# A mixer, differential attention and a second mixer on one core: the order of the first block, and which queue loads the low-rank weights

## The chip, the cores and the metric

One NeuronCore of one Trainium2 chip runs the whole program in one launch. The metric is the time on the device in us, the median over the runs shown. "TensorE" is PE in the rows, "VectorE" DVE, "ScalarE" ACT, "Pool" POOL, and "SP" the queue of the sync engine, which only issues transfers here.

## The reference

The input x has 256 tokens of 2048 channels. Layer A is an RWKV-7 mixer with a residual layer norm, layer B differential attention with another, block C a sparse attention and retention mixer with a squared-relu MLP. The change lies in layer A alone, up to its eighth head group:

```
xx = shift(x) - x
xs = x[None] + xx[None] * mu_proj[:, None, None, :]
r, k, v, g = einsum('sbtd,sde->sbte', xs, w_in)
xw = x + xx * mu_lora[0];  xa = x + xx * mu_lora[1]
w_log = -softplus(-(w0 + tanh(xw @ w1) @ w2)) - 0.5;  decay = exp(-exp(w_log))
a  = sigmoid(a0 + (xa @ a1) @ a2)
kk = normalised(k * k_k);  k = k * (1 + (a - 1) * k_a)
S_t = S_{t-1} diag(w_t) - (S_{t-1} kk_t) (a_t*kk_t)^T + v_t k_t^T ;  y_t = S_t r_t
y = groupnorm(y) + bonus;  x = layernorm(ALPHA * x + (y * silu(g)) @ w_out)
```

All of it is float32; the kernel makes each product with the weights from two float32r parts of both sides.

## The kernel before

Activations are kept transposed, each as a high part xh and a low part xl. `dense` (L210) makes one block of 512 output columns for both token tiles of 128. SP loads the raw weights in pairs of k-tiles, 512 KB each, into four buffers. For each of the 16 k-tiles ScalarE casts the high part wh (L221), VectorE subtracts it to get the low part wl (L222), both with four buffers, and TensorE makes six products (L230, L231, L232 for each token tile): 96 products to a block. Between k-tiles `dense` calls a hook and takes pieces of other work from two lists, `soon` and `side`.

Layer A has 16 blocks: r (0 to 3), k (4 to 7), v (8 to 11) and g (12 to 15). The mixed input of the r blocks is made ahead of and beside block 0 by `mixed` (L419): pairs of k-tiles are mixed from x and from the steps xxg by two operations on VectorE (ms, L410), cast by ScalarE (xh, L166) and subtracted by VectorE (xl, L167). Pool makes three of the four granules of xxg (L399, L400). The low-rank hidden layers tanh(xw @ w1) and xa @ a1 are sixteen pieces in `side` (`low_rank`, L486), which run from block 1 on: each loads 128 KB of weights, issued by ScalarE (L488), casts and splits them (L490, L491), mixes a pair of k-tiles and makes six products.

Beside the v and g blocks run eight head groups ("head 0" to "head 7", four heads each). `wkv_prepare` loads rkl (r, k and kk, 768 KB) and w2 ([97, 2, 256], 194 KB), makes zp, the product of the hidden layer with w2 (L602), the sigmoid sig (ScalarE L605, VectorE L606), its parts sh and sl (L608, L609), the sums over chunks (L618 with the mask tri, a cast of trif), the decays E, then KB and ZR, the masked products AT (L662, L664), and the blocks of the inverse. These pass through DRAM to Pool, which substitutes (L690, L692), and come back as xd; L733 is the first product that needs them. The third mixed input, for the g blocks, is made again from x, which `mixed_again` loads in pairs (xt, L446) for VectorE's xx (L448).

A tile scheduler orders the instructions of each engine, apart from those marked to be kept in program order, and places transfers and casts ahead of the place where they stand in the program when their buffers are free. In the kernel before, nothing below was marked: the loads by ScalarE of tables, id16, trif, kkb, rkl and w2 could be moved ahead.

Of the kernel before, what the change touches and what calls it, by code (L numbers as in the profile page):

```python
# [17 lines left out]
D = 2048  # L18
T = 256
# [7 lines left out]
PLAN = 203.0            # weight of the steps of the heads over the blocks beside which they are put  # L27
SP = ((0.0, 0.2), (0.2, 0.8), (0.6, 0.8))     # their parts of a period
PAUSE = 8.0             # weight of the step that waits for the value blocks
AHEAD = 2               # pairs of k-tiles that are mixed before the first block  # L30
LAG = 10                # k-tiles by which the first token tile leads in the blocks around a norm


# ---------------------------------------------------------------- constants of the shapes
def const_tables():
# [13 lines left out]
    # distance of query and key, very large where the chunk mask forbids the pair  # L49
# [7 lines left out]
    # rotary tables, token-major  # L57
# [5 lines left out]
    # retention decay, key rows by query columns: blocks (0,0) (0,1) (1,1)  # L63
# [15 lines left out]
    # T5 buckets of the distances 255 - i, one-hot; row 32 marks the masked (negative) ones  # L79
# [16 lines left out]
def body(tc, I, out, dbg=None, stop=99):  # L96
# [3 lines left out]
    with ExitStack() as ctx:  # L100
# [29 lines left out]
        def load(pool, name, src, shape, eng=None, **kw):  # L130
            t = pool.tile(shape, F32, tag=name, name=name, **kw)
            (eng or S).dma_start(t, src)
            return t

        def bc_rows(src, n):
            """An AP that reads the n contiguous values at src for each of 128 partitions."""
            return bass.AP(tensor=src.tensor, offset=src.offset, ap=[[0, 128], [1, n]])
# [4 lines left out]
        S.copy(warm, mhalf)                         # the activation tables come in beside the first loads  # L142
        lnc = cst.tile([128, 15, KT], F32, name="lnc")              # vectors by channel

        def rpow(dst, src, n):
            """dst = src ** -0.5 for a few values per partition."""
            G.tensor_tensor(dst, src, mhalf.to_broadcast([128, n]), op=OP.pow)
# [4 lines left out]
        # ------------------------------------------------ matrix products with the weights  # L152
        class HL:
            """Activations, transposed, as two float32r parts whose sum is the float32 value."""
# [14 lines left out]
        def tok_to_hl(hlx, g, src, tts=(0, 1)):  # L169
            """src: token-major [128, 2, 512]; fills granule g."""  # L170
# [15 lines left out]
        def stepped(steps):  # L186
            """The steps of a generator, one at a time, as work for `side`."""

            def go():
                if next(steps, "end") is None:  # L190
                    side.insert(0, go)

            return go

        def in_turn(gens):
            """The steps of several generators, each a step behind the one before."""
# [12 lines left out]
        def dense(hlx, w, n=512, ks=None, hook=None):  # L209
            """One block of output columns, for both token tiles; returns the two PSUM tiles.  # L210
            Between its steps it emits the work that stands in `soon`, then in `side`."""
# [26 lines left out]
        # ------------------------------------------------ norms between products  # L238
        def norm_between(hlo, w, evac, finish, hlx, src, gain, offset, w_next, wp):
            """The four blocks hlo @ w, a norm of the rows that leads to src, and hlx = src * gain + offset  # L240
            (by channel) with the first block hlx @ w_next, whose PSUM tiles it returns.
            evac(tt, j, acc) takes a block in, finish(tt) makes src for one token tile."""
# [35 lines left out]
        def residual_ln(res_block, dst):  # L278
            """The two functions of norm_between for the layer norm of (ALPHA * residual + block)."""
# [19 lines left out]
        def gain_rows(dst, gain, offset, after=None):  # L299
            """dst = dst * gain + offset in place, row by row; gain and offset by their quarters of columns."""  # L300
# [12 lines left out]
        def rows_of(tiles, src):  # L313
            """Rows of D values broadcast over the partitions, in the given places; returns its quarters."""
# [5 lines left out]
        def pairs(t):  # L320
            """The 512-wide pairs that fit in a tile, as places for split weights."""
# [5 lines left out]
        def lag_block(hlx, w, store, hooks, place=0):  # L327
            """One block of output columns, the first token tile some k-tiles ahead of the second, so that
            what follows from one token tile runs beside the products of the other. store holds split weights."""
# [38 lines left out]
        # ================================================ layer A: RWKV-7  # L368
        vo = res.tile([128, 2, D], F32, tag="r1", name="vo")          # v, then the mixer's output
# [5 lines left out]
        with ExitStack() as actx:  # L375
# [5 lines left out]
            # the input, channel-major, and the steps to the tokens before; the places are the heads' later  # L381
# [37 lines left out]
            def mixed(which, ahead=8):  # L419
                """The mixed input in two parts. Returns it and a hook for the first block that uses it,  # L420
                which makes the parts beyond the first `ahead` pairs of tiles."""
                hx = HL()

                def pair(q):
                    if q % 2 == 0:
                        hx.alloc(q // 2)
                    split_from(hx, q // 2, slice(2 * (q % 2), 2 * (q % 2) + 2), slice(0, T), mix_pair(which, q))

                left = list(range(ahead, 8))
                calls = [0]  # L430

                def hook():
                    calls[0] += 1
                    if left and calls[0] % 2:
                        pair(left.pop(0))

                for q in range(ahead):
                    pair(q)
                return hx, hook

            def mixed_again(which):
                """The same when the input has left its places."""
# [15 lines left out]
            # r, k and the normalised k * k_k: channel-major, kept in DRAM until their heads come up  # L458
            rkd = [da.tile([128, 3, 4, T], F32, name=f"rkd{j}") for j in range(4)]
            hx, ahead = mixed(0, AHEAD)  # L460
# [19 lines left out]
            # low-rank hidden layers, rank by token, a few products at a time between those of the blocks  # L480
# [4 lines left out]

            def low_rank(q, li):  # L486
                w1 = ap1.tile([128, 2, 128], F32, tag="pr", name="lw1")
                S.dma_start(w1, I[("w1", "a1")[li]][:, 2 * q:2 * q + 2])  # L488
                wp = ap1.tile([128, 2, 2, 128], FR, tag=("f", "tha")[li], name="lwp")
                S.copy(wp[:, 0], w1)  # L490
                V.tensor_sub(wp[:, 1], w1, wp[:, 0].bitcast(F32))  # L491
# [15 lines left out]
            r_block(0, ahead)  # L507
# [11 lines left out]
            V.tensor_scalar(a0h, lnc[:, 12], 0.5, None, op0=OP.mult)  # L519
            V.tensor_scalar(kah, lnc[:, 13], 0.5, None, op0=OP.mult)  # L520
            V.tensor_scalar(kab, kah, -1.0, 1.0, op0=OP.mult, op1=OP.add)
            rkm = ap1.tile([128, KT, 2], F32, name="rkm")
            V.memset(rkm, 0.0)
            V.tensor_copy(rkm[0:64, :, 0], lnc[0:64, 14])
            V.tensor_copy(rkm[64:128, :, 1], lnc[64:128, 14])
# [3 lines left out]
            def k_block(j):  # L529
                acc = dense(hx, I["w_k"][j])  # L530
                kkb = ap1.tile([128, 512], F32, tag="xx", name="kkb")
                S.dma_start(kkb, bc_rows(I["k_k"][512 * j:512 * j + 512], 512))
# [32 lines left out]
            # v: token-major  # L565
# [14 lines left out]
            S.dma_start(trif, I["consts"][:, _OFF["tri"][0]:_OFF["mask_a"][0]])  # L580
            S.copy(tri, trif)
            # block-diagonal inverses pass through DRAM; the zeros around the blocks are written once
# [959 lines left out]
```

## Time and profile before

| | us |
|---|---|
| median of 3 runs | 2468.78 |
| lowest, highest | 2464.99, 2470.33 |
| span of the profiled execution, first to last instruction | 2472.8 |
| TensorE busy in it | 2392.2 (97%), 12378 matmuls |
| VectorE busy | 1540.1 (62%) |
| ScalarE busy | 1240.3 (50%) |
| Pool busy | 322.1 (13%) |

The mean granted clock of TensorE over the profiled execution is 0.983 of full speed. The span of the profiled execution is 4.0 us longer than the median of the runs; its own time on the device, what lies around the span included, is not among the times shown. In the page's table by 40 slices of 61.8 us TensorE is busy six tenths of the first slice and of the fifth (from 247 us), eight tenths of two others, and nine or more of the rest. The rows are read so: a stretch is found in the table of windows, the cause of a gap in the bracket behind the row that ends it, and the time of a transfer in the views of the transfers.

### The profile page before, as it was taken

What the parts mean: (1) busy time and instruction counts of PE and PEld (TensorE: products, weight loads), DVE (VectorE), ACT (ScalarE), POOL (GpSimd) and SP (SyncE); (2) the same over time, 40 slices, a digit from 0 to 9 for tenths busy, and PEclk for the clock granted to TensorE, in tenths of its full rate; (3) what the DMA queues carried; (4) which work ended last, traced back from release to release, by engine and by line L of the source; (5) the groups of instructions that cost most, each with busy time, mean ns of one, the idle gap of its engine ahead of it and who ended that gap; (6) DMA issues with size and microseconds to landing.
All of it is one profiled execution on the core that took longest, in us unless ns stands there. A gap on an engine that the chain in (4) does not pass through costs nothing.

```text
span 2472.8 us, 34618 instructions
## 1 busy us (share of the span) xinstructions
PE 2392.2 (97%) x12378; PEld 1940.8 (78%) x12378; DVE 1540.1 (62%) x2679; ACT 1240.3 (50%) x2540; POOL 322.1 (13%) x455
## 2 busy tenths in 40 slices
PE   6999699999999999999989999999999999999998
PEld 4887577777787788888878887878788888888886
DVE  6777466655466755776575477665655555556555
ACT  3555343435446455555464445455655555445443
POOL 1013244334400400100030011000000000000001
PEclk9999898989999999999999999999999999999999
DMA  5777534444365766546656754456566666666664
GB/s 183 213 231 253 146 96 125 121 103 96 95 208 179 216 189 194 145 145 182 198 179 197 243 150 137 128 174 210 166 184 186 187 189 186 187 187 187 187 188 154
DMA packets 155862, 428.08 MB, mean 173 GB/s; under 512 B 47110, under 2 KB 51294, under 8 KB 155049
## 3 DMA queue, kind: packets, MB, share of 16 engines
q1 hardware_dynamic: 139680, 386.84, 53.3%
q0 software_dynamic: 6128, 23.65, 3.3%
q10 hardware_dynamic: 9880, 15.39, 2.0%
q8 instruction: 97, 1.59, 0.3%
q14 instruction: 77, 0.62, 0.1%
HBM read 413.20 MB, written 14.18 MB: 173 GB/s over the span
## 4 chain that ended last, share of the span: by engine, by line
PE 88%; DVE 5%; DMA 3%; issue 1%; ACT 1%; POOL 1%; POOLq 0%; DVEq 0%; SPq 0%; ACTq 0%
PE acc L230 24%; PE acc L231 23%; PE acc L232 23%; PE m L150 3%; PE acc L341 2%; PE acc L339 2%; PE acc L340 2%; PE m L733 1%; PE m L662 1%; DVE wl L222 1%; PE m L776 1%; PE m L801 1%; PE m L765 1%; PE m L769 1%; DMA lw<-in_a 1%
## 5 line engine op out<-in xcount | busy, mean ns | idle before, releaser
L222 DVE TENSOR_TENSOR wl<-raw,wh 128x512 fp32r<-128x512 f32 x1312 | 916.8, 703 | 694.6 <-ACT wh L221 690.9
L221 ACT CAST wh<-raw 128x512 fp32r<-128x512 f32 x1312 | 811.8, 621 | 878.7 <-PE acc L232 524.3
L230 PE MATMUL acc<-wh,xh 128*128 128x512 f32 x2624 | 1058.3, 403 | 18.1 <-ACT wh L221 18.1
L231 PE MATMUL acc<-wl,xh 128*128 128x512 f32 x2624 | 1036.5, 395 | 9.4 <-DVE wl L222 9.4
L232 PE MATMUL acc<-wh,xl 128*128 128x512 f32 x2624 | 1036.7, 395 | 0.0
L230 PEld LDWEIGHTS acc<-wh,xh 128*128 128x128 f32 x2624 | 495.8, 189 | 128.5 <-ACT wh L221 20.1
L231 PEld LDWEIGHTS acc<-wl,xh 128*128 128x128 f32 x2624 | 496.8, 189 | 115.4 <-DVE wl L222 12.8
L232 PEld LDWEIGHTS acc<-wh,xl 128*128 128x128 f32 x2624 | 495.8, 189 | 110.9 <-issue 0.9
L1447 POOL TENSOR_TENSOR dn<-dn,gd 128x512 f32<-128x512 f32 x6 | 9.4, 1578 | 672.0 <-ACT jk L1446 672.0
L690 POOL TENSOR_TENSOR pr<-A,X 64x15 f32<-64x15 f32 (+7 forms) x120 | 50.2, 418 | 197.8 <-DMA A<-d 189.2
L359 DVE TENSOR_TENSOR lw<-raw,lw 128x512 fp32r<-128x512 f32 x84 | 56.4, 700 | 29.9 <-ACT lw L358 29.5
L358 ACT CAST lw<-raw 128x512 fp32r<-128x512 f32 x84 | 50.4, 629 | 42.8 <-PE acc L341 28.0
L341 PE MATMUL acc<-lw,xl 128*128 128x512 f32 x168 | 67.6, 402 | 3.8 <-DVE xl L167 3.7
L339 PE MATMUL acc<-lw,xh 128*128 128x512 f32 x168 | 68.7, 409 | 2.3 <-ACT xh L166 2.3
L340 PE MATMUL acc<-lw,xh 128*128 128x512 f32 x168 | 67.0, 399 | 0.0
L772 ACT COPY Q<-m 64x256 f32<-64x256 f32 x32 | 11.8, 368 | 79.1 <-PE m L769 75.9
L662 PE MATMUL m<-ZR,KB 64*128 64x128 f32 x256 | 39.7, 311 | 6.2 <-DVE KB L647 6.2
L662 PEld LDWEIGHTS m<-ZR,KB 64*128 64x128 f32 x256 | 33.0, 208 | 14.0 <-issue 7.9
L692 POOL TENSOR_TENSOR X<-X,pr 64x15 f32<-64x15 f32 (+7 forms) x120 | 42.0, 350 | 9.2
L341 PEld LDWEIGHTS acc<-lw,xl 128*128 128x128 f32 x168 | 32.1, 191 | 13.1 <-DVE xl L167 6.1
L167 DVE TENSOR_TENSOR xl<-m,xh 128x512 fp32r<-128x512 f32 (+1 forms) x60 | 36.7, 648 | 8.3 <-ACT xh L166 8.2
L339 PEld LDWEIGHTS acc<-lw,xh 128*128 128x128 f32 x168 | 32.2, 191 | 9.6 <-ACT xh L166 3.5
(349 smaller groups left out, 2195.5 us busy)
## 6 DMA issues: line engine op xcount, KB each, us to landing
raw<-in_w_up SPq DMA_DIRECT2D x128, 512.0 KB, 3.7
raw<-in_w_down SPq DMA_DIRECT2D x128, 512.0 KB, 3.7
raw<-in_w_in SPq DMA_DIRECT2D x104, 512.0 KB, 4.1
raw<-in_w_qg SPq DMA_DIRECT2D x64, 512.0 KB, 3.7
raw<-in_w_r SPq DMA_DIRECT2D x32, 512.0 KB, 4.4
raw<-in_w_k SPq DMA_DIRECT2D x32, 512.0 KB, 4.3
raw<-in_w_v SPq DMA_DIRECT2D x32, 512.0 KB, 3.6
raw<-in_w_g SPq DMA_DIRECT2D x32, 512.0 KB, 4.0
```

What stands on the lines that cost most here:

```text
L150: PE.transpose(dst, src, ident[:n, :n])
L221: S.copy(wh, r[:, i])
L222: V.tensor_sub(wl, r[:, i], wh.bitcast(F32))
L230: PE.matmul(o, a, wh, start=first, stop=False)
L231: PE.matmul(o, a, wl, start=False, stop=False)
L232: PE.matmul(o, b, wh, start=False, stop=last)
L339: PE.matmul(acc[tt], a, wh, start=k == 0, stop=False)
L340: PE.matmul(acc[tt], a, wl, start=False, stop=False)
L341: PE.matmul(acc[tt], b, wh, start=False, stop=k == KT - 1)
L358: S.copy(wh, raw[:, step % 2])
L359: V.tensor_sub(wl, raw[:, step % 2], wh.bitcast(F32))
L662: PE.matmul(p[:, ci], KB[hb, ct, tt, 2 * eo:2 * eo + 2], ZR[hb, ct, tt, 2 * eo:2 * eo + 2], start=True, stop=True)
```

## The change

Four things change, all in layer A; elsewhere comments are removed, so that line numbers differ by 2 near the start and by 16 to 19 from the k blocks on.

1. One pair of k-tiles is mixed before block 0 instead of two, and the rest is mixed half a pair for each k-tile: the mix and ScalarE's cast in one step, VectorE's subtraction in the next.
2. VectorE's order is fixed by hand for `mixed(0)` and for block 0.
3. The sixteen loads of low-rank weights by ScalarE become three by Pool: w1 whole (1 MB) and a1 in halves (512 KB each), ahead of block 0.
4. The ScalarE loads `tables`, `id16`, `rkl` and `w2`, the casts of the low-rank weights and of tri, and some small constants are kept in program order. kkb and trif are loaded by Pool, in program order too.

```diff
-AHEAD = 2
+AHEAD = 1
 def load(pool, name, src, shape, eng=None, **kw):
-    (eng or S).dma_start(t, src)
+    d = (eng or S).dma_start(t, src)
+    if eng is None:
+        tc.keep_in_program_order(d)
 ...
 def pair(q):
     if q % 2 == 0:
         hx.alloc(q // 2)
-    split_from(hx, q // 2, slice(2 * (q % 2), 2 * (q % 2) + 2), slice(0, T), mix_pair(which, q))
-left = list(range(ahead, 8))
+    ks = slice(2 * (q % 2), 2 * (q % 2) + 2)
+    h, l = hx.h[q // 2][:, ks], hx.l[q // 2][:, ks]
+    ms = mix_pair(which, q)
+    S.copy(h, ms)
+    yield
+    V.tensor_sub(l, ms, h.bitcast(F32))
+left = [s for q in range(ahead, 8) for s in [pair(q)] * 2]
 def hook():
-    calls[0] += 1
-    if left and calls[0] % 2:
-        pair(left.pop(0))
+    if left:
+        next(left.pop(0), None)
 ...
-hx, ahead = mixed(0, AHEAD)
+with tc.manual_schedule(engines={V.engine}):
+    hx, ahead = mixed(0, AHEAD)
 ...
+lw = [[ap1.tile([128, KT, 128], F32, tag="AT2", name="lww")],
+      [ap1.tile([128, KT // 2, 128], F32, tag=t_, name="lwa") for t_ in ("xd", "VU")]]
+def low_rank_weights():
+    tc.keep_in_program_order(G.dma_start(lw[0][0], I["w1"]))
+    for i in range(2):
+        tc.keep_in_program_order(G.dma_start(lw[1][i], I["a1"][:, 8 * i:8 * i + 8]))
 def low_rank(q, li):
-    w1 = ap1.tile([128, 2, 128], F32, tag="pr", name="lw1")
-    S.dma_start(w1, I[("w1", "a1")[li]][:, 2 * q:2 * q + 2])
+    n = KT // len(lw[li])
+    w1 = lw[li][2 * q // n][:, 2 * q % n:2 * q % n + 2]
 ...
-r_block(0, ahead)
+low_rank_weights()
+with tc.manual_schedule(engines={V.engine}):
+    r_block(0, ahead)
 ...
-    S.dma_start(kkb, bc_rows(I["k_k"][512 * j:512 * j + 512], 512))
+    tc.keep_in_program_order(G.dma_start(kkb, bc_rows(I["k_k"][512 * j:512 * j + 512], 512)))
 ...
-S.dma_start(trif, I["consts"][:, _OFF["tri"][0]:_OFF["mask_a"][0]])
-S.copy(tri, trif)
+tc.keep_in_program_order(G.dma_start(trif, I["consts"][:, _OFF["tri"][0]:_OFF["mask_a"][0]]))
+tc.keep_in_program_order(S.copy(tri, trif))
 ...
-    rkl = load(ap2, "rkl", rkd[gi // 2][:, :, u], [128, 3, 2, T], S)
-    w2 = load(ap2, "w2", I["w2"][:, :, cols], [97, 2, 256], S)
+    rkl = load(ap2, "rkl", rkd[gi // 2][:, :, u], [128, 3, 2, T])
+    w2 = load(ap2, "w2", I["w2"][:, :, cols], [97, 2, 256])
```

VectorE at the start, before: from the first mixed pairs to the first two low parts of the weights (a0h, kah, kab and rkm are small constants of the heads).

```order
L410 SCALAR_TENSOR_TENSOR ms_131<-xxg_105,lnc_85,xg_95 128x256 x2
L410 SCALAR_TENSOR_TENSOR ms_136<-xxg_105,lnc_85,xg_95 128x256 x2
L519 TENSOR_SCALAR a0h_1115<-lnc_85 128x16
L520 TENSOR_SCALAR kah_1116<-lnc_85 128x16
L524 COPY rkm_1121<-lnc_85 64x16
L525 COPY rkm_1121<-lnc_85 64x16
L521 TENSOR_SCALAR kab_1117<-kah_1116 128x16
L410 SCALAR_TENSOR_TENSOR ms_162<-xxg_110,lnc_85,xg_95 128x256 x2
L167 TENSOR_TENSOR xl_130<-ms_131,xh_129 128x512
L167 TENSOR_TENSOR xl_130<-ms_136,xh_129 128x512
L222 TENSOR_TENSOR wl_151<-raw_148,wh_150 128x512
L167 TENSOR_TENSOR xl_161<-ms_162,xh_160 128x512
```

VectorE at the same place in the change:

```order
L412 SCALAR_TENSOR_TENSOR ms_133<-xxg_105,lnc_85,xg_95 128x256 x2
L435 TENSOR_TENSOR xl_132<-ms_133,xh_131 128x512
L224 TENSOR_TENSOR wl_157<-raw_154,wh_156 128x512
L412 SCALAR_TENSOR_TENSOR ms_166<-xxg_105,lnc_85,xg_95 128x256 x2
L224 TENSOR_TENSOR wl_171<-raw_154,wh_170 128x512
L435 TENSOR_TENSOR xl_132<-ms_166,xh_131 128x512
L224 TENSOR_TENSOR wl_184<-raw_181,wh_183 128x512
L412 SCALAR_TENSOR_TENSOR ms_195<-xxg_110,lnc_85,xg_95 128x256 x2
L224 TENSOR_TENSOR wl_200<-raw_181,wh_199 128x512
L435 TENSOR_TENSOR xl_194<-ms_195,xh_193 128x512
L224 TENSOR_TENSOR wl_213<-raw_210,wh_212 128x512
```

The first low part wl now follows one mixed pair and its xl, the constants are gone from here, and each further wl stands behind at most one pair of ms or one xl.

ScalarE in block 0, before (w is w2, of heads 0 and 1; lw a low-rank weight):

```order
L132 DMA id_2258<-in_consts 64x256
L221 CAST wh<-raw 128x512
L166 CAST xh<-ms 128x512
L132 DMA w_2400<-in_w 97x2x256
L221 CAST wh<-raw 128x512
L132 DMA w_2583<-in_w 97x2x256
L166 CAST xh<-ms 128x512
L221 CAST wh<-raw 128x512
```

No transfer is issued there in the change. These issues stand in its v blocks; ScalarE at the end of the first 10 k-tiles of block 8, in the change (w is w2 of head 0):

```order
L600 CAST tri<-trif 128x256
L223 CAST wh<-raw 128x512
L132 DMA rkl<-rkd_125 128x3x512
L132 DMA w_2380<-in_w 97x2x256
L223 CAST wh<-raw 128x512 x3
L453 DMA xt<-in_xT 128x512
L223 CAST wh<-raw 128x512
L453 DMA xt<-in_xT 128x512
L624 ACTIVATE sig<-m 128x512
```

The issues of rkl and w2 of head 0 went from block 0 and block 5 to a place behind the cast of tri and four weight casts ahead of sig. For the heads behind it w2 is likewise issued three to six weight casts ahead of its sig, where before it was 16 to 25 casts ahead (for heads 0 and 1 over 130). On TensorE the order from zp to L618 of head 0 is unchanged: 12 products with the weights stand between them.

## Rows read from the trace of the kernel before

**Rows 1.** The table of windows: busy time of each engine (with its count of instructions) in some stretches from the span's start, in us; PEclk is the granted clock of TensorE, then the share of the transfer engines' time and GB/s.
```profile
40.00:50.00 10.00, 5.79 (x12) 3.76 (x12) 2.99 (x6) 2.50 (x5) 0.00 (x0) 0.66 0.28 83
...
100.00:240.00 140.00, 140.00 (x688) 116.92 (x687) 115.01 (x200) 85.67 (x156) 33.13 (x30) 1.00 0.74 236
240.00:250.00 10.00, 5.33 (x25) 4.06 (x23) 3.36 (x7) 2.20 (x4) 0.56 (x1) 1.00 0.88 282
...
290.00:300.00 10.00, 0.00 (x0) 0.00 (x0) 0.00 (x0) 0.00 (x0) 5.13 (x14) 0.55 0.22 37
```

**Rows 2.** The timeline of TensorE from 0 to 60 us: start, duration, engine, line, operation, out<-in by the program's names, count, and in brackets the idle time before it and what ended it.
```profile
15.61 0.80 PE L231 MATMUL acc<-wl,xh 128*128 128x512 f32 x1 [4.93 <-DVE wl L222]
...
42.52 0.79 PE L230 MATMUL acc<-wh,xh 128*128 128x512 f32 x1 [5.06 <-ACT wh L221]
...
56.58 0.60 PE L150 MATMUL m<-c_ident,ev 128*128 128x128 f32 x4
```

**Rows 3.** The timeline of ScalarE from 0 to 60 us, with the same columns; ACTq is ScalarE's issue of a transfer.
```profile
8.79 0.62 ACT L221 CAST wh<-raw 128x512 fp32r<-128x512 f32 x1
...
34.11 7.64 ACTq L488 DMA_DIRECT2D lw<-in_a  x1
41.85 1.14 ACT L221 CAST wh<-raw 128x512 fp32r<-128x512 f32 x2 [7.53 <-issue]
...
49.27 0.40 ACT L490 CAST lwp<-lw 128x256 fp32r<-128x256 f32 x1 [5.02 <-DMA lw<-in_a]
```

**Rows 4.** The timeline of VectorE from 0 to 50 us, with the same columns.
```profile
5.68 2.45 DVE L410 SCALAR_TENSOR_TENSOR ms<-xxg,lnc,xg 128x256 f32<-128x256 f32 x4
...
10.35 1.72 DVE L410 SCALAR_TENSOR_TENSOR ms<-xxg,lnc,xg 128x256 f32<-128x256 f32 x2
...
14.04 1.52 DVE L222 TENSOR_TENSOR wl<-raw,wh 128x512 fp32r<-128x512 f32 x1
...
16.09 1.28 DVE L222 TENSOR_TENSOR wl<-raw,wh 128x512 fp32r<-128x512 f32 x2
17.29 0.87 DVE L410 SCALAR_TENSOR_TENSOR ms<-xxg,lnc,xg 128x256 f32<-128x256 f32 x2
```

**Rows 5.** The timeline of Pool, with the same columns: its last step (xxg) at the start, and its last multiplication of the k blocks.
```profile
14.98 0.65 POOL L400 TENSOR_SCALAR xxg<-xg 128x2 f32<-128x2 f32 x1
...
236.91 1.04 POOL L557 TENSOR_TENSOR k<-k,ss 128x512 f32<-128x512 f32 x1
```

**Rows 6.** The timeline of TensorE around the first head, with the same columns: L602 is zp, L618 the first product that needs sig, L733 the first product that needs the inverse.
```profile
241.49 1.03 PE L602 MATMUL m<-w,hw 97*128 97x256 f32 x4
...
252.77 0.79 PE L618 MATMUL m<-tri,sh 128*128 128x256 f32 x2 [7.44 <-ACT sh L608]
...
301.90 0.44 PE L733 MATMUL m<-xd,AT 64*64 64x64 f32 x2 [13.82 <-DMA xd<-d]
```

**Rows 7.** The chain of waits around the first head: start, us, engine and line; and two products behind the stall before L733.
```profile
240.35 10.52 DMA xt<-in_xT
...
309.44 0.43 PE acc L232
309.87 0.23 PE acc L230
```

**Rows 8.** The timeline of ScalarE at its issue of w2 for head 5.
```profile
364.30 0.68 ACTq L132 DMA_DIRECT2D w<-in_w  x1
```

**Rows 9.** The view of the transfers from 364 to 376 us: GB/s in 40 equal slices of 0.3 us, and what ScalarE's queue (q10) moved: packets, MB, share of 16 engines' time.
```profile
GB/s 0 0 0 0 0 0 0 14 24 14 0 3 20 24 24 27 24 24 24 24 20 24 24 20 24 20 24 20 79 20 24 20 24 24 20 24 20 38 123 123
...
q10 hardware_dynamic: 195, 0.20, 5.3%
```

**Rows 10.** The view of the transfers over the whole span: issuing queue, count, KB of one, median us from issue to landing.
```profile
rkl<-rkd ACTq DMA_DIRECT2D x8, 768.0 KB, 8.1
...
trif<-in_consts ACTq DMA_DIRECT2D x1, 128.0 KB, 5.0
```

**Rows 11.** The timeline of TensorE: zp of heads 3 to 7.
```profile
356.20 1.03 PE L602 MATMUL m<-w,hw 97*128 97x256 f32 x4
...
410.15 1.03 PE L602 MATMUL m<-w,hw 97*128 97x256 f32 x4
...
466.80 1.03 PE L602 MATMUL m<-w,hw 97*128 97x256 f32 x4
...
513.16 1.03 PE L602 MATMUL m<-w,hw 97*128 97x256 f32 x4
...
567.19 1.13 PE L602 MATMUL m<-w,hw 97*128 97x256 f32 x4
```

**Rows 12.** The timeline of ScalarE: for heads 3 to 7 the last instruction behind a product of TensorE ahead of the place where the changed program issues w2 (in head 5 a cast, which stands behind two copies of a block's products).
```profile
344.26 0.37 ACT L772 COPY Q<-m 64x256 f32<-64x256 f32 x1 [2.90 <-PE m L769]
...
399.49 0.37 ACT L777 COPY VU<-m 64x256 f32<-64x256 f32 x1 [0.31 <-PE m L776]
...
462.29 0.65 ACT L166 CAST xh<-ms 128x512 fp32r<-128x512 f32 x1
...
501.08 0.37 ACT L772 COPY Q<-m 64x256 f32<-64x256 f32 x1 [4.90 <-PE m L769]
...
555.25 0.37 ACT L772 COPY Q<-m 64x256 f32<-64x256 f32 x1 [2.45 <-PE m L769]
```

**Rows 13.** The page's costliest groups: line, engine, operation, out<-in, count | busy, mean ns of one | idle time before it and what ended most of it.
```profile
L662 PE MATMUL m<-ZR,KB 64*128 64x128 f32 x256 | 39.7, 311 | 6.2 <-DVE KB L647 6.2
```

More of the change, by code (lines that the diff above doesn't have):

```diff
@@ L426, in pair @@
                         hx.alloc(q // 2)
-                    split_from(hx, q // 2, slice(2 * (q % 2), 2 * (q % 2) + 2), slice(0, T), mix_pair(which, q))
-                left = list(range(ahead, 8))
-                calls = [0]
+                    ks = slice(2 * (q % 2), 2 * (q % 2) + 2)
[5 more added lines that the diff above has]
+                left = [s for q in range(ahead, 8) for s in [pair(q)] * 2]
                 def hook():
-                    calls[0] += 1
-                    if left and calls[0] % 2:
-                        pair(left.pop(0))
+                    if left:
+                        next(left.pop(0), None)
                 for q in range(ahead):
-                    pair(q)
+                    for _ in pair(q):
+                        pass
                 return hx, hook
@@ L484, in body @@
             pt = [mbank(256), mbank(256)]
+            lw = [[ap1.tile([128, KT, 128], F32, tag="AT2", name="lww")],
[4 more added lines that the diff above has]
+                    tc.keep_in_program_order(G.dma_start(lw[1][i], I["a1"][:, 8 * i:8 * i + 8]))
             def low_rank(q, li):
-                w1 = ap1.tile([128, 2, 128], F32, tag="pr", name="lw1")
-                S.dma_start(w1, I[("w1", "a1")[li]][:, 2 * q:2 * q + 2])
+                n = KT // len(lw[li])
+                w1 = lw[li][2 * q // n][:, 2 * q % n:2 * q % n + 2]
                 wp = ap1.tile([128, 2, 2, 128], FR, tag=("f", "tha")[li], name="lwp")
-                S.copy(wp[:, 0], w1)
-                V.tensor_sub(wp[:, 1], w1, wp[:, 0].bitcast(F32))
+                tc.keep_in_program_order(S.copy(wp[:, 0], w1))
+                tc.keep_in_program_order(V.tensor_sub(wp[:, 1], w1, wp[:, 0].bitcast(F32)))
                 ms = mix_pair(4 + li, q)
@@ L518, in body @@
             kab = ap1.tile([128, KT], F32, name="kab")
-            V.tensor_scalar(a0h, lnc[:, 12], 0.5, None, op0=OP.mult)
-            V.tensor_scalar(kah, lnc[:, 13], 0.5, None, op0=OP.mult)
+            tc.keep_in_program_order(V.tensor_scalar(a0h, lnc[:, 12], 0.5, None, op0=OP.mult))
+            tc.keep_in_program_order(V.tensor_scalar(kah, lnc[:, 13], 0.5, None, op0=OP.mult))
             V.tensor_scalar(kab, kah, -1.0, 1.0, op0=OP.mult, op1=OP.add)
             rkm = ap1.tile([128, KT, 2], F32, name="rkm")
-            V.memset(rkm, 0.0)
-            V.tensor_copy(rkm[0:64, :, 0], lnc[0:64, 14])
-            V.tensor_copy(rkm[64:128, :, 1], lnc[64:128, 14])
+            tc.keep_in_program_order(V.memset(rkm, 0.0))
+            tc.keep_in_program_order(V.tensor_copy(rkm[0:64, :, 0], lnc[0:64, 14]))
+            tc.keep_in_program_order(V.tensor_copy(rkm[64:128, :, 1], lnc[64:128, 14]))
             hx, _ = mixed(1)
```

## The prediction

> **What bounds the kernel now.** I read the table of windows first, to find the stretches in which TensorE is not busy, then the timelines of the engines in those stretches, the chain of waits, and last the views of the transfers. TensorE is busy in 140.00 of the 140 us from 100 to 240 [rows 1], so there an edit to ScalarE, VectorE or a queue is worth nothing. Two places touched by the change are different. In the first block of products the windows show 5.79 us busy of 10 from 40 to 50, at a granted clock of 0.66. Around the first head they show 5.33 of 10 from 240 to 250, and 0.00 from 290 to 300. After 300 TensorE is nearly full again, but a head has no spare there: what makes TensorE wait lengthens the program.
>
> In the first block the reader is to see three holes in TensorE's timeline [rows 2]: 4.93 us before 15.61, waiting for the first low part wl; 5.06 before 42.52, waiting for a weight cast; and the transposes that stand 12 products after the block, only at 56.58. ScalarE's timeline says whose they are [rows 3]: the issue of one low-rank load took 7.64 us from 34.11, the next weight cast then showed 7.53 us of "issue", and at 49.27 a cast had waited 5.02 us for that load. VectorE's timeline explains the first [rows 4]: two mixed pairs, small constants and two xl stand ahead of the first wl at 14.04. Beside Pool, which works on the steps until 14.98 + 0.65 = 15.6 [rows 5], a pair of ms takes 1.72 us and a wl 1.52; alone they take 0.87 and 0.64.
>
> **Block 0: a gain.** By the new vector order, wl comes after one ms pair and one xl. Four ms took 2.45 us from 5.68 [rows 4], so the first pair ends near 6.9; its cast (0.62) and xl (at most 1.52) end near 9.0. The weight cast was at 8.79 + 0.62 = 9.4 [rows 3], and is no later now. Then, at the slow prices beside Pool: wl to 10.9, ms pair to 12.7, wl to 14.2, xl to 15.7. From there at the fast prices: 14 wl by 0.64, 6 xl at about the same 0.64, 12 ms by 0.87 / 2, in all 9.0 + 3.8 + 5.2 = 18.0, so VectorE ends near 33.7. TensorE needs 6 products more, 1.4 us at a warm pitch of 0.23, and 12 more (2.8) to the transposes: 37.9 instead of 56.58, a gain of 18.7. I take **-17.5**, since one low-rank piece still stands in that stretch and TensorE starts at the slow pitch of 0.43 [rows 7]. Bounds: -19; and, if the 2 MB of Pool loads take from the weights what the landing of one 768 KB load is now, 8.1 us [rows 10], -9.5.
>
> Sixteen loads fewer on ScalarE are nothing beyond that: their casts lie from 60 to 240, where TensorE is full [rows 1]. The three loads stand behind the steps on Pool, from 15.6; the first cast that reads them comes in block 1, after 35, some 20 us later, against 8.1 for 768 KB. That is the cover; if it fails, ScalarE waits and weight casts with it. The Trainium skill (DMA: Bandwidth & Descriptors, "Issuing engines are not separate DMA queues") says that another issuing engine saves only the sequencer's time, usually small. By that rule only the 4.9 us before 15.61 [rows 2] would be left of block 0's gain and the sum be +21; by the row, where the issue itself held ScalarE for 7.64 us [rows 3], it is as above, and I go by the row.
>
> kkb and trif move to Pool's queue, behind what stands there. kkb is needed a block later: nothing. trif is not.
>
> **Head 0: a loss.** Before, w2 of heads 0 and 1 was loaded in block 0, and zp, the product that reads it, ran at 241.49 without a wait [rows 6]. What TensorE then waited for was sig, behind a step on VectorE that waited for xt, 10.52 us from 240.35 [rows 7], until 252.77. Now ScalarE casts tri before it issues rkl and w2. tri needs trif, which Pool issues after its last multiplication, 236.91 + 1.04 = 238.0 [rows 5]; trif landed in 5.0 [rows 10], so 243.0, and w2 goes out at 243.5.
>
> How long does w2 take? Its issue of 364.30 [rows 8] is followed by a rate of 24 GB/s, flat, until some 11.2 us after the issue, in which its queue moved 195 packets and 0.20 MB [rows 9]. The transfer alone is 0.20 MB / 24 GB/s = 8.3 us, and its packets took 5.3% of 16 engines' 12 us, 10.2 us of one: I read that as a transfer that runs on one engine. With rkl right ahead in the same queue, 768 KB / 16 = 48 KB stand before it on that engine: 2.0 us. I take 13.2 from issue to landing; bounds 11.2 (rkl costs nothing) and 18 (contention such as made xt's 256 KB take 10.52).
>
> So zp comes at 256.7. Between zp and the next product that waits for sig stand the same 12 weight products as before, now after a stall, at the slow pitch: 0.9 + 12 x 0.43 = 6.1, so 262.8 instead of 252.77. ScalarE and VectorE's way (sig, sh, three steps of 0.6 or less) runs beside them, and xt, a few casts later, is there by then. From 252.77 the chain to 301.90 is 49 us of products, transfers and Pool's substitution, and unchanged: **+10** (bounds +5 and +15). Heads 1 and 2 also wait for w2 now, but lie inside that chain, where TensorE idles 13.82 us before 301.90 [rows 6]: nothing.
>
> **Heads 3 to 7: a loss.** Before, w2 was loaded far ahead. Now its issue stands in program order, 3 to 6 weight casts ahead of its sig. The last thing ScalarE does before the issue stands behind products of TensorE, so the lead is from there to zp in the old times [rows 11, 12]: head 3, 344.26 + 0.37 to 356.20, 11.6; head 4, 399.49 + 0.37 to 410.15, 10.3; head 5, 462.29 + 0.65 to 466.80, 3.9; head 6, 501.08 + 0.37 to 513.16, 11.7; head 7, 555.25 + 0.37 to 567.19, 11.6. Against 13.2 that leaves 1.6, 2.9, 8.0 (in head 5 only an xt of 256 KB is right ahead, 16 KB on that engine, so 11.9), 1.5 and 1.6: **+16**. Bounds: with 11.2 for all, 0.9 + 7.3, +8; and, if each of five waits is followed by some 13 products at 0.43 for 0.23, 2.6 more each, +29.
>
> **The sum.** -17.5 + 10 + 16 = +8.5. The sum is against one execution with a span of 2472.8 us; the runs shown have a median of 2468.78, and I add to that: **2477**. 0.2% (4.9 us) is about what a measurement of this kernel can tell from no change.
>
> **Rivals.** *Faster: the new waits take the place of old ones.* TensorE already waits for VectorE in the heads (KB, 6.2 us in all [rows 13]), and a wait for w2 lets VectorE and Pool catch up. If w2 lands within the 10.3 us lead of head 4, only head 5 waits (11.9 less 2.9 less 3.9, 5); head 0 loses 10 less 2.9, 7, and some 3 are given back: -17.5 + 7 + 5 - 3 = -8.5, 2460. It decides at a landing of 10.3. For it: the old leads of 10 to 12 are close to the landing. Against it: the flat rate, 8.3 us before any latency. Chance 0.23.
>
> *Balance.* Landing near 11.2 and head 0 at +8: -17.5 + 8 + 8 = -1.5, so 2467, and up to 2473 with a little of the slow pitch. Chance 0.2.
>
> *The clock.* Each stall brings the slow pitch behind it, as 0.43 us products stand behind the stall before 301.90 [rows 7]: 13 more, 2490. Part of the slower side, 0.15.
>
> *Block 0 gains less.* Pool's loads come late or press on the weights: 8 less, 2485. The Trainium skill (SBUF — State Buffer, "SBUF: two separate sides") says that work on VectorE can keep Pool from writing the descriptors of its loads. No row here shows it. If the loads came 8 us after the first cast that reads them, ScalarE would wait as at 49.27 [rows 3] and 8 of the gain be lost. Chance 0.07.
>
> *The change doesn't do what it says*: ScalarE in block 0 waits for another thing where the issue stood, and only the 4.9 us before the first wl are gained (what the rule on issuing engines would give): -4.9 + 10 + 16 = +21, 2490. Chance 0.05.
>
> **How the numbers follow.** The forecast itself (2474 to 2484) has 0.3. With the clock, the smaller gain and the order that misses, slower by over 0.2% has 0.57; same 0.2; faster 0.23. The likeliest case's own range is 2474 to 2484; the 8 in 10 reach from the middle of the faster case to past the clock's: 2459 to 2494.
>
> **What would show it.** In the profile after: the transposes behind block 0 near 38, not 56.6, and no "issue" wait of ScalarE in the first 60 us; TensorE waiting at zp for the DMA of w2 in head 0 until about 239 (257 less the gain); in head 5 some 8 us, in the others 1 to 3; the xt wait of head 0 gone from the chain. I am wrong if zp waits for nothing in heads 3 to 7, if w2 lands within 10 us of its issue, or if block 0 still ends past 45.

## The result, and the profile after

The changed kernel takes 2495.97 us (median of 4 runs, 2491.39 to 2497.34) against 2469.56 for the kernel before (2464.99 to 2471.89): ratio 1.0102, interval 1.0087 to 1.0117. It is slower by some 25 us. The forecast was slower by 8, with a range up to 2494: the direction held, the size did not. Medians and ratios here and below leave out two executions, one of the kernel before at 8176.27 us and one of the kernel with the order alone at 2586.46.

The two profiled executions have spans of 2472.8 and 2489.6 us, 16.8 apart. The end of each block's products on ScalarE (its copy out of PSUM) and three products of head 0 cut both traces at the same places. First the table of windows of the kernel before: block 0; blocks 1 to 7; head 0 up to the first product that needs sig; from there to the first that needs the inverse; to the end of block 9; blocks 10 and 11 (zp of heads 3 and 4 stands there); block 12 (of heads 5 and 6); blocks 13 and 14 (of head 7).

```profile
0.00:52.91 52.91, 30.21 (x98) 22.06 (x99) 33.41 (x63) 18.57 (x33) 10.24 (x17) 0.93 0.58 180
52.91:228.32 175.41, 175.41 (x853) 146.76 (x852) 141.71 (x249) 103.25 (x187) 26.60 (x25) 0.99 0.74 232
228.32:252.77 24.45, 17.01 (x84) 13.66 (x82) 14.60 (x28) 10.65 (x21) 8.41 (x8) 0.94 0.69 217
252.77:301.90 49.13, 35.31 (x205) 29.89 (x205) 26.36 (x48) 17.77 (x35) 15.33 (x34) 0.85 0.48 125
301.90:324.14 22.24, 22.24 (x204) 17.36 (x205) 11.08 (x19) 8.52 (x18) 12.99 (x33) 0.86 0.50 138
324.14:461.34 137.20, 132.40 (x1039) 104.22 (x1037) 82.47 (x148) 56.54 (x172) 48.15 (x87) 0.91 0.45 116
461.34:514.91 53.57, 53.57 (x488) 42.62 (x487) 33.54 (x63) 29.20 (x92) 30.88 (x59) 1.00 0.48 126
514.91:637.76 122.85, 119.39 (x983) 93.04 (x981) 72.29 (x119) 50.94 (x155) 56.87 (x95) 0.94 0.42 98
```

The same stretches of the changed kernel:

```profile
0.00:36.81 36.81, 24.82 (x94) 18.00 (x95) 29.66 (x53) 18.17 (x31) 12.18 (x19) 1.00 0.78 278
36.81:211.76 174.95, 174.95 (x856) 146.50 (x855) 143.55 (x258) 103.34 (x187) 27.90 (x29) 1.00 0.69 214
211.76:251.43 39.67, 20.45 (x84) 15.94 (x82) 14.11 (x24) 10.93 (x21) 9.82 (x10) 0.74 0.58 163
251.43:304.95 53.52, 34.76 (x204) 29.29 (x203) 28.48 (x52) 18.05 (x35) 15.11 (x34) 0.86 0.45 119
304.95:327.60 22.65, 22.65 (x206) 17.51 (x207) 11.87 (x20) 9.20 (x18) 11.08 (x29) 0.87 0.39 109
327.60:463.57 135.97, 127.47 (x1037) 100.20 (x1036) 76.54 (x142) 55.01 (x168) 50.04 (x99) 0.95 0.47 114
463.57:529.61 66.04, 55.76 (x489) 43.88 (x488) 37.37 (x67) 30.36 (x93) 31.56 (x60) 0.95 0.45 120
529.61:654.92 125.31, 119.74 (x983) 93.35 (x982) 71.01 (x119) 51.07 (x155) 49.92 (x86) 0.95 0.44 103
```

The reader is to see: block 0 takes 36.81 us for 52.91, a gain of 16.1; blocks 1 to 7 the same (-0.5). Head 0 up to sig takes 39.67 for 24.45, a loss of 15.2, and its chain 53.52 for 49.13, a loss of 4.4. Blocks 10 and 11 lose nothing (-1.2), block 12 loses 12.5, blocks 13 and 14 lose 2.5; the stretch between the chain and the end of block 9 loses 0.4. To the end of block 14 the sum is 17.2, and the rest gives back 0.4. The timeline of TensorE in the changed kernel, the lines that answer to [rows 2], [rows 6] and [rows 11], says what stands in the lossy stretches:

```profile
40.01 0.60 PE L152 MATMUL m<-c_ident,ev 128*128 128x128 f32 x4
...
246.06 2.05 PE L621 MATMUL m<-w,hw 97*128 97x256 f32 x4 [16.33 <-DMA w<-in_w]
...
251.43 0.51 PE L637 MATMUL m<-tri,sh 128*128 128x256 f32 x2
...
280.05 2.05 PE L621 MATMUL m<-w,hw 97*128 97x256 f32 x4 [10.34 <-DMA w<-in_w]
...
304.95 0.44 PE L752 MATMUL m<-xd,AT 64*64 64x64 f32 x2 [7.71 <-DMA xd<-d]
...
362.39 2.05 PE L621 MATMUL m<-w,hw 97*128 97x256 f32 x4 [2.63 <-DMA w<-in_w]
...
417.14 2.05 PE L621 MATMUL m<-w,hw 97*128 97x256 f32 x4 [4.59 <-DMA w<-in_w]
...
478.21 2.05 PE L621 MATMUL m<-w,hw 97*128 97x256 f32 x4 [7.74 <-DMA w<-in_w]
...
527.77 1.10 PE L621 MATMUL m<-w,hw 97*128 97x256 f32 x4 [2.54 <-DMA w<-in_w]
...
578.66 1.10 PE L621 MATMUL m<-w,hw 97*128 97x256 f32 x4 [1.99 <-DMA w<-in_w]
```

The transposes behind block 0 stand at 40.01 (forecast 38; before 56.58), and zp of head 0 at 246.06 (forecast 239). At zp (L621) TensorE waits for the DMA of w2 in seven of the eight heads: 16.33, 10.34, 2.63, 4.59, 7.74, 2.54 and 1.99 us. The chain of waits gives the landings, from issue to the last byte:

```profile
225.03 20.90 DMA w<-in_w
...
272.75 7.36 DMA A<-d
...
347.98 14.27 DMA w<-in_w
...
401.41 15.60 DMA w<-in_w
...
464.70 13.38 DMA w<-in_w
...
513.42 14.21 DMA w<-in_w
...
564.64 13.88 DMA w<-in_w
```

In the kernel before, the same chain has this for A<-d, the blocks of the inverse on their way to Pool:

```profile
275.18 2.80 DMA A<-d
```

The timeline of ScalarE shows that what stands behind w2 is held too: the issue of xt behind it took 11.67 us, and a weight cast waited 11.23 for "issue", where before it was an issue of 0.33.

```profile
224.42 0.58 ACTq L132 DMA_DIRECT2D rkl<-rkd  x1
...
225.03 1.23 ACTq L132 DMA_DIRECT2D w<-in_w  x1
...
228.00 11.67 ACTq L453 DMA_DIRECT2D xt<-in_xT  x1
239.79 0.62 ACT L223 CAST wh<-raw 128x512 fp32r<-128x512 f32 x1 [11.23 <-issue]
```

### The profile page after: what moved, and what is told of

Its sections match the earlier page's. It is cut to its first block, busy times and chain, and to the rows that moved or that the text cites. A ratio compares the mean times of both kernels' runs of the same rounds, so it can differ in the third digit from the quotient of the medians.

```text
span 2489.6 us, 34589 instructions
## 1 busy us (share of the span) xinstructions
PE 2387.7 (96%) x12378; PEld 1935.3 (78%) x12378; DVE 1534.3 (62%) x2679; ACT 1242.6 (50%) x2540; POOL 323.2 (13%) x463
## 4 chain that ended last, share of the span: by engine, by line
PE 85%; DMA 6%; DVE 5%; issue 1%; ACT 1%; POOL 1%; SPq 0%; ACTq 0%; DVEq 0%; POOLq 0%
PE acc L232 23%; PE acc L233 22%; PE acc L234 22%; DMA w<-in_w 4%; PE m L152 3%; PE acc L343 2%; PE acc L342 2%; PE acc L341 2%; PE m L681 1%; DVE wl L224 1%; PE m L752 1%; PE m L784 1%; PE m L795 1%; PE m L788 1%; PE m L820 1%
## 5 line engine op out<-in xcount | busy, mean ns | idle before, releaser
L709 POOL TENSOR_TENSOR pr<-A,X 64x15 f32<-64x15 f32 (+7 forms) x120 | 41.8, 348 | 220.8 <-DMA A<-d 212.1
L621 PE MATMUL m<-w,hw 97*128 97x256 f32 x32 | 13.6, 567 | 46.2 <-DMA w<-in_w 46.2
L621 PEld LDWEIGHTS m<-w,hw 97*128 97x128 f32 x32 | 7.9, 274 | 50.0 <-issue 48.8
```

## The experiments

Each kernel is shown by its edit, to the changed kernel or to the kernel before. Ratios are to runs of the kernel before on the same chip; kernels that stand in one group below did not always run on the same one.

**The shape of w2.** To the changed kernel:

```diff
-w2 = load(ap2, "w2", I["w2"][:, :, cols], [97, 2, 256])
+w2 = ap2.tile([97, 2, 256], F32, tag="w2", name="w2")
+tc.keep_in_program_order(S.dma_start(w2[:96], I["w2"][:96, :, cols]))
+tc.keep_in_program_order(S.dma_start(w2[96:97, 0], I["w2"][96:97, 0, cols]))
```

> The changed kernel, with w2 loaded in two transfers, 96 rows and the 97th alone. Theory 1 (a transfer over 97 rows runs on one transfer engine, and the wait for it is what the heads lose): the waits of TensorE at zp for w2 go from 46 us in seven heads to under 15 us in all, w2 lands within 9 us of its issue instead of 13 to 21, A<-d of head 0 comes back from 7.4 towards 3 us; the time falls by 20 to 30 us, to 2466 to 2476. Theory 2 (w2 is late because rkl and other transfers stand before it, whatever its shape): landing stays above 12, the waits above 35 us, the time above 2488.

Measured 2442.61, ratio 0.9914 (0.9884 to 0.9944): 53 us below the changed kernel by the medians, 46 by the ratios, and faster than the kernel before. The issues stand where they stood; the shape differs (and 1 KB of the 97th row that no product reads is left out). The timeline of TensorE at zp of head 0, the chain of waits at head 0, then the view of the transfers over the whole span:

```profile
236.01 1.62 PE L623 MATMUL m<-w,hw 97*128 97x256 f32 x3 [4.81 <-DMA w<-in_w]
```

```profile
225.46 10.46 DMA w<-in_w
...
261.98 2.68 DMA A<-d
```

```profile
w<-in_w ACTq DMA_DIRECT2D x8, 192.0 KB, 6.0
```

Only heads 0 and 1 wait for w2 now (4.81 and 1.30 us). The 96 rows land in 6.0 us (median), where 97 rows took 13.4 to 20.9; in head 0 the chain has 10.46 for 20.90. A<-d of head 0 took 2.68 us instead of 7.36. The packets in the changed kernel's trace say why: 960 of its 1024 had started by 275.1, and the last 64, one sixteenth, started from 277.8 to 279.7, one engine's share, while the last packets of w2 of head 1 started up to 279.4. The time came out 23 us below the range that I had expected, and the waits at zp fell by 40, the time by 46 to 53: the w2 transfers cost more than the waits that bear their name. In the view of the transfers of the changed kernel, from 347 to 362 us, the reader sees how such a transfer looks, after 4.5 us in which rkl's 768 KB pass: 22 to 25 GB/s, interrupted by others, until the landing at 362.25.

```profile
GB/s 175 67 51 222 202 289 366 333 360 197 120 60 25 25 25 25 22 22 153 98 243 350 330 224 55 22 33 14 27 27 27 19 22 188 55 251 339 426 150 55
```

The packets agree: the 194 of w2, of 1 KB each, go nearly always one at a time from 351.2 to 361.5, where rkl ahead of them had up to 19 in flight. So the 97 rows run on one engine, as forecast from [rows 9]. The Trainium skill (DMA: Bandwidth & Descriptors, "Why a DMA increments its semaphore by 16 and not by 1") says that such a transfer is split over the largest number of engines, up to 16, that divides the slowest dimension of both sides: 16 for 96 partitions. By that rule 97 leave one engine; the traces agree, with a flat 24 to 25 GB/s and a landing of 13.4 to 20.9 us against 6.0.

**The order alone of rkl and w2.** To the kernel before:

```diff
-rkl = load(ap2, "rkl", ..., S)
-w2 = load(ap2, "w2", ..., S)
+rkl = load(ap2, "rkl", ..., S, keep=True)      # load() then calls tc.keep_in_program_order
+w2 = load(ap2, "w2", ..., S, keep=True)
```

> The kernel before, with nothing changed but that rkl and w2 are kept in program order. Theory 1: head 0 loses some 15, its chain 4, heads 5 to 7 some 15, less what block 0 gains without the two issues of w2 (up to 5): plus 25 to 35, 2494 to 2505. Rival (the losses of the change come from trif and kkb on Pool's queue): under plus 10, below 2480.

Measured 2500.26, ratio 1.0163 (1.0109 to 1.0217). The waits at zp are those of the changed kernel (15.27, 11.76, 2.64, 4.38, 7.41, 2.30 and 2.01 us), so this part of the change alone brings the loss. It also showed what I had not forecast: with the issues of w2 gone from block 0, and its order and loads as before, block 0 ends at 38.54 and block 7 at 213.32, 15.0 earlier than before. And the reverse, the changed kernel with `S` passed to both loads again, so that they may be issued ahead:

> The changed kernel, with rkl and w2 free to be issued ahead as before; everything else of the change stays. Theory 1 (the whole loss is the late issue of w2): the gain of block 0 (16.6 us) stays, no wait at zp, 2449 to 2457, faster than both. Rival (the gain of block 0 is lost in the heads anyway, by Pool and VectorE, whatever w2 does): 2465 or more. Between: the two issues of w2 are back in block 0 and hold ScalarE there as before, 2457 to 2465.

Measured 2460.05, ratio 0.9995 (0.9966 to 1.0024), the middle case: no wait at zp, but w2 is issued at 11.2 and 12.6 us, block 1 ends at 67.7 instead of 61.6, and block 7 at 217.88 instead of 211.76. So 6.1 of the 16.6 us of early gain went with it.

**What made block 0 shorter.** Four more, each to the kernel before: one pair ahead, half pairs and the fixed order of VectorE alone; the three early Pool loads alone; w2 in two transfers alone; and the first with the third. The diffs are those of the change and the split above.

> The kernel before with the new mixing of block 0 alone (one pair ahead, half pairs, VectorE's order fixed); the low-rank weights still come in sixteen loads on ScalarE's queue. If the order and the loads each give their part: the first hole of 4.9 us goes, the 5.06 behind the issue of a low-rank load stays, 2460 to 2466. If the order alone gives block 0's gain: 2451 to 2455. If it gives nothing without the loads: 2467 to 2472.

> The kernel before with the three early loads of low-rank weights by Pool, and nothing else. Theory 3 (the holes of block 0 are made by w2's transfers): the hole behind the issue of a low-rank load goes, but w2 still takes the one engine that the weights of block 0 need too, so block 0's columns are copied out between 42 and 50 us and the time is 2458 to 2470. If the sixteen loads were the cause: 40 or earlier, 2450 to 2458.

> The kernel before with w2 in two transfers, 96 rows and one, and nothing else. Theory 3: the low-rank load no longer waits behind w2's transfers, block 0's columns are copied out by 42 us instead of 52.9, and the time falls by 10 to 20, to 2450 to 2460. Rival (block 0 is held by the low-rank loads or by VectorE's order): 50 or later, 2465 or more.

> The kernel before with the new mixing and order of block 0 and w2 in two transfers, free to be issued ahead; sixteen low-rank loads on ScalarE. If shape and order are all that counts, it is as fast as the changed kernel with the two transfers (2442.6) or faster, since w2 is never waited for: 2434 to 2446. If the early Pool loads are worth something of their own: 2450 or more.

Measured: order 2453.77, ratio 0.9953 (0.9920 to 0.9986); Pool loads 2465.85, 0.9997 (0.9973 to 1.0021); split 2452.65, 0.9918 (0.9882 to 0.9954); order and split 2451.51, 0.9914 (0.9883 to 0.9946). The last lies in the range that I had kept for Pool's loads being worth something, but its ratio is that of the changed kernel with w2 split, so that is not shown. The timeline of ScalarE has the end of block 0 and of block 7 in each, here of order, Pool loads, split, and both:

```profile
42.56 0.59 ACT L482 COPY ev<-acc 128x512 f32<-128x512 f32 x1
...
217.91 0.58 ACT L556 COPY k<-acc 128x512 f32<-128x512 f32 x1
```

```profile
45.13 1.07 ACT L477 COPY ev<-acc 128x512 f32<-128x512 f32 x2
...
219.66 0.58 ACT L559 COPY k<-acc 128x512 f32<-128x512 f32 x1
```

```profile
39.67 1.06 ACT L477 COPY ev<-acc 128x512 f32<-128x512 f32 x2
...
213.97 0.58 ACT L550 COPY k<-acc 128x512 f32<-128x512 f32 x1
```

```profile
36.28 1.07 ACT L482 COPY ev<-acc 128x512 f32<-128x512 f32 x2
...
211.04 0.58 ACT L556 COPY k<-acc 128x512 f32<-128x512 f32 x1
```

Against 52.91 and 228.32 before, block 7 ends 10.4, 8.7, 14.4 and 17.3 us earlier; in the changed kernel 16.6. The gains do not add: beside the split the order is worth 2.9, alone 10.4. I read it so that each part alone makes room around the two transfers of w2; with Pool's loads alone, for one, no low-rank load stands behind w2, which is issued only at 29.40 and 30.89 instead of 22.34 and 23.69. The view of the transfers of the kernel before, from 20 to 45 us, shows it; each column is 0.625 us.

```profile
GB/s 123 197 337 296 197 175 334 207 120 33 108 84 220 234 249 23 25 25 23 23 106 167 370 228 133 239 306 164 80 25 23 23 23 21 23 26 179 57 106 128
```

Two stretches at 21 to 26 GB/s, some 3 and 4 us long, are what is left visible of the two w2 transfers of block 0 beside the weights. The low-rank load that took 7.64 us to issue and was waited for [rows 3] stood behind them in the same queue. With w2 split, the same load is issued in 0.36 us, and the cast behind it waits 1.92.

**Sixteen loads or three.** The changed kernel with `low_rank` loading its 128 KB on ScalarE again:

> The changed kernel with the low-rank weights again in sixteen loads of 128 KB on ScalarE's queue; rkl, w2, trif, kkb and VectorE's order stay as changed. Theory 3 (the holes of block 0 came from the two transfers of w2 that stood in ScalarE's queue, not from the low-rank loads): block 0's columns are copied out by 39 us, as with Pool's loads (36.8), and the time is that of the changed kernel, 2488 to 2499. Rival (my forecast: the issue of low-rank loads held ScalarE): the copy comes after 42, the time is 2500 or more.

Measured 2502.42, ratio 1.0138 (1.0086 to 1.0189). Block 0 ends at 36.23: with w2 out of it, Pool's loads give it nothing. But block 7 ends at 221.98, 10.2 later than in the changed kernel: the casts of these weights are now kept in order right behind their loads, and wait for them 15 times, 40.3 us in all on ScalarE. So the rival of this expectation has the right total and the wrong place. The early loads are worth 10 us at the end of block 7, and only because the change pins the casts: with sixteen loads and free casts (order and split, above) block 7 ends at 211.04.

**Which step of head 0.** The changed kernel with w2 issued before rkl, and the one with trif loaded and cast behind the r blocks:

```diff
+w2 = load(ap2, "w2", I["w2"][:, :, cols], [97, 2, 256])
 rkl = load(ap2, "rkl", rkd[gi // 2][:, :, u], [128, 3, 2, T])
 rj, kg, kkg = rkl[:, 0], rkl[:, 1], rkl[:, 2]
-w2 = load(ap2, "w2", I["w2"][:, :, cols], [97, 2, 256])
```

> The changed kernel with w2 issued right before rkl instead of right behind it. If rkl's share of the one engine is what makes w2 land at 13.4 to 15.6 instead of 11.2: w2 lands within 9 to 12 of its issue, the waits at zp of heads 3, 6 and 7 go (2 to 2.6 us each), the 46 us of waits fall to 20 to 30, and the time falls by 5 to 15. If rkl, now behind w2 on that engine, is late in turn: zp waits less but KB and ZR wait for rkl, and the time stays within 5 of the changed kernel.

> The changed kernel with trif loaded and cast behind the r blocks; w2 as changed, over 97 rows and behind rkl. If trif on Pool's queue is what makes head 0 late: w2 goes out 5 us or more earlier and the time falls by 5 to 10. If w2's own landing is (my present theory): the issue moves by under 3 us, the wait at zp of head 0 stays above 12, and the time stays within 4 of the changed kernel, 2486 to 2500.

w2 first: 2467.71, ratio 0.9999 (0.9980 to 1.0017), 20 below the changed kernel on the same chip, more than I had expected; waits at zp are left in heads 0 (12.54), 1 (9.43) and 5 (3.79), 25.8 us in all. In head 0 w2, now ahead of rkl, still took 17.46 us to land. tri early: 2495.01, 1.0129 (1.0066 to 1.0193); the wait of head 0 is 16.36, and w2, issued at 223.01 instead of 225.03, took 21.59 to land. trif is not the cause; the landing is.

**The best of these.**

> The changed kernel with w2 in two transfers and trif loaded and cast behind the r blocks. If the wait of 4.8 us at zp in head 0 hangs on trif: it goes, and the time is 3 to 6 below the 2442.6 of the two transfers alone. If it hangs on the full transfer engines (rkl, xt and the rest at 400 GB/s): the wait stays above 3, and the time changes by less than 2.

> The changed kernel with w2 in two transfers and rkl and w2 free to be issued ahead. If what was found adds up: block 0 ends at 36 to 38, no wait at zp, and the heads run as with the two transfers; 2430 to 2442, a ratio of 0.983 to 0.990 to the kernel before, the fastest of all. If the four issues of w2 in block 0 still cost what they did there: 2445 or more.

The changed kernel with w2 split and tri early took 2441.37, ratio 0.9877 (0.9839 to 0.9915), the fastest ratio of the study. The wait at zp of head 0 stayed (5.63), so it does not hang on trif; that it hangs on the other transfers at that place is what is left, not shown. Against the split alone the 1.2 us are within what can be told. With w2 split and free to be issued ahead the time was 2457.50, 0.9952 (0.9936 to 0.9968): no wait at zp, blocks 0 to 7 as good (211.98), and yet 15 above the split alone by the medians, 9 by the ratios (on another chip). My expectation missed. Its heads wait for KB, 1.9 to 2.4 us in four of them, and run at a lower granted clock, as those of the kernel before do; with the split in program order two such waits are left (2.69 and 1.04). What takes them away I have not isolated. Issuing ahead by itself does not bring them: the kernel before with w2 split issues ahead too, and its profile has two waits for KB (1.91 and 1.26) and 294.1 us for blocks 10 to 14, as w2 split in program order has (294.2), against 312.6 here.

**The measured pair again.**

> The changed kernel again, beside the others on one chip: 2489 to 2500 if the first measurement holds, ratio 1.008 to 1.014.

> The kernel before, unchanged, for a second profile. The waits that the profile names in the heads (KB, xt, xd) are the same to within 1 us; if the time differs by up to 18 us from the first, the difference lies in the heads, in stretches at the lower granted clock, and the mean granted clock differs with it (0.991 at 2453, 0.984 at 2470).

> The kernel before, unchanged, for a third profile; as the second.

The changed kernel again: 2488.16, ratio 1.0103 (1.0056 to 1.0149). The kernel before gave 2461.66 and 2470.55. The windows from 324 us to the end of block 11 in the first of these:

```profile
324.00:388.00 64.00, 61.89 (x519) 48.31 (x518) 37.95 (x63) 26.38 (x83) 24.70 (x42) 1.00 0.47 116
388.00:454.50 66.50, 64.03 (x520) 50.73 (x518) 44.35 (x84) 29.67 (x89) 23.93 (x46) 0.92 0.48 129
```

against 137.20 us at 0.91 in the first profile. The waits for KB in it are 1.95, 2.32, 1.91 and 1.26 us; the first profile has 2.19, 1.91 and 1.27, and one of 1.41 for AT. What differs is the granted clock: blocks 10 to 14 take 301.1 us there and 313.6 in the first profile, and blocks 0 to 9 agree within a microsecond or two. The profiled execution of the kernel before was one of its longer ones, that of the changed kernel the shortest of four. That is why the traces differ by 16.8 us and the medians by 26.

## Why the prediction was wrong

- **Block 0, -17.5:** measured -16.1; the size is right. The reason was half wrong. I put the second hole down to the issue of a low-rank load and the gain to Pool's loads and VectorE's order. Each alone does bring part of the gain while w2 stands in the block (8.7 and 10.4 us at the end of block 7). But what held the issue was w2, ahead in the same queue: its move or its split alone gives 14 to 15 of the 16.6, the order adds 2 to 3 to that, and Pool's loads then add nothing in block 0. They hide 10 us of new waits in blocks 1 to 7. So the right size is in part luck. That w2 goes out of block 0 I counted only as a loss. "No issue wait of ScalarE in the first 60 us" held.
- **Head 0, +10:** measured +15.2 and, in the chain that I called unchanged, +4.4. This is the step that failed first: "I take 13.2 from issue to landing". It was 20.9 in head 0, beyond my bound of 18, and 13.4 to 15.6 in heads 3 to 7. In the 13.2, rkl's share of the engine was 2.0 us, as if rkl had it alone, and the transfer itself was taken at the 8.3 us of an undisturbed one. In head 0 the first packet of w2 started 7.6 us after the issue, and the packets then took 12.7 us; in heads 3 to 7 it was 2.1 to 4.2 and 10.2 to 10.9. With w2 ahead of rkl the whole time falls by some 20 us, but head 0's landing is still 17.46. Around head 0 rkl, two pairs of weights, gn, kkT and xt were in flight as well. The 4.4 is A<-d, 7.36 us for 2.80 before, a sixteenth of it on the engine that w2 of head 1 held: a cost for others that my sum had no term for, as was ScalarE held 11.23 us by xt's issue. The xt wait of head 0 did go from the chain, as forecast.
- **Heads 1 and 2, 0:** held, but for A<-d. TensorE waited 10.34 us at zp of head 1 and 6.1 us less for xd.
- **Heads 3 to 7, +16:** measured +13.7 in the profiled pair, but not where I put it. Waits of 2.63 and 4.59 in heads 3 and 4 (forecast 1.6 and 2.9) cost nothing in this pair: TensorE idles 3.7 us more there, since waits for VectorE (1.41 and 2.19) are gone, and is busy 4.9 us less, with the granted clock at 0.95 for 0.91; 7.74 and 2.54 in heads 5 and 6 (forecast 8.0 and 1.5) cost 12.5 in block 12, 2.2 more than themselves, with the clock at 0.95; 1.99 in head 7 (forecast 1.6) stands in blocks that lost 2.5. Against the second profile of the kernel before (2459.9), blocks 10 and 11 lost 4.9 us and heads 3 to 7 in all 26, near the upper bound of 29 that I gave for waits followed by the slow pitch.
- **The sum, +8.5:** 16.8 in the profiled pair, 26 by the medians. In the pair the sum is 8.3 too low: head 0 and its chain lost 9.6 more than I said, block 0 gained 1.4 less, and heads 3 to 7 and the rest lost some 2.7 less. The other 9.6 up to the medians comes from which executions were profiled: I set my sum against one execution, and that one was itself long. Of the rivals, the two at 2490 ("the clock" and "the change doesn't do what it says") came nearest, in number only: what was missed first is the landing. The range ended at 2494, too low.
- **The rivals:** "new waits take the place of old ones" holds in half for heads 3 and 4 (7.2 us of new waits, 3.7 more idle); its condition, a landing of 10.3, was not met. The one on Pool's descriptors did not occur: w1's 1 MB landed in time for every cast. The Trainium skill's rule on issuing engines (DMA: Bandwidth & Descriptors, "Issuing engines are not separate DMA queues") would have given 2490. The sequencer was held 7.64 us before and 11.67 after, in both cases behind a transfer on one engine, so its "usually small" didn't hold for these two; but with w2 out of block 0, Pool's issuing was worth nothing there (36.81 against 36.23), as the rule says.

## What to carry to other kernels

Look at the shape of a transfer before its place. One over 97 rows ran at 24 GB/s and held up what shared its engine: its own reader, the loads behind it in the queue, the issuing engine, and other queues' transfers. Ninety-six rows and one cost an issue more and were worth some 50 us in the changed kernel and 20 in the kernel before, more than all the reordering.

A hole that ends with a transfer isn't always that transfer's: ask what stood ahead of it in its queue, and test by changing that alone. And where executions of one kernel differ by 20 us, make the sum against several profiles.

## What the runs showed that I had not expected

- The issue of a transfer behind one on a single engine could take long: 4.86 and 7.64 us in the kernel before, 11.67 in the changed one and 13.16 in its second profile. With w2 split, no issue of ScalarE in the first 700 us of the changed kernel took more than 1.3.
- Pool's 1 MB load of w1 landed in 5.4 us, issued at 16.31, though VectorE was busy 9.83 us of the 10 from 10 to 20 us and 9.20 of the next 10.
- Executions of the kernel before on one chip took 2452 to 2479 us, with mean granted clocks from 0.992 to 0.981. Two of its profiles (2459.9 and 2468.8) have nearly the same waits and differ by 9 us.
